# First projection of an encoder trunk: keys, values and the first q group in one pass of 512 columns

## The chip, the cores and the metric

The kernel runs on one core of a Trainium2 chip. Its time is the device time of one execution in microseconds; lower is better. Matmuls run on TensorE (PE, with its weight loads as PEld), elementwise work on VectorE (DVE), ScalarE (ACT) and GpSimd (POOL); nearly all transfers are issued by SyncE (SP).

## The reference, cut to what matters

Two sequences (1024 and 512 tokens, width 1024) go through the same two layers. Only the beginning of layer 0 is changed:

```
z = rmsnorm(x, g) @ w_in          # qa 512 | ka 128 | va 128 | ga 512 | mixer B 1536 columns
qa = rotate_pairs(rmsnorm(qa per head, gain0), ang) * 64**-0.5    # 8 heads of 64
ka = rotate_pairs(rmsnorm(ka per head, gain1), ang)               # 2 heads of 64
oa = dense_gqa(qa, ka, va)        # per sequence, 4 query heads share a key head
ob = rmsnorm(retention forwards + backwards of the mixer B columns)
x  = x + concat(silu(ga) * oa, silu(gb) * ob) @ w_out
```

Layer 1 has windowed attention with its own projections, and a last RMSNorm follows. Everything is float32.

## The kernel before, in words

The 1536 tokens are 12 blocks of 128, in three groups (t = 0, 1, 2) of four; group 2 is the second sequence. x arrives transposed: for each group t and each k of 8 pieces of the width there is a tile of 128 features by 512 tokens. `load_xt` scales it by g and splits it into a rounded part `xh` (ACT; POOL for group 2) and a rest `xl` (DVE, L118). The norm's factor `rs` (one per token) does not depend on the projection: `block_stats` (L388) reads x a second time, sums squares on ACT (L177), and takes the power on POOL (L103); `rs` is multiplied in when results leave PSUM, or later.

Weights come in chunks of 256 columns (`CW`). `load_w` (L130) loads two k of a chunk at once (128 x 512, rows of 2 KB), and POOL splits each such tile into a rounded part (L139) and a rest (L140), so a chunk is four tiles. They live in two sets of four slots, tags "w" and "wg"; their raw form has two slots (`wraw`), or, for the first chunk, slots of the general tag "E" (12).

A projection `proj_tm_k` (L150) of one block and one k is three matmuls into PSUM: xh by the weights' rounded part, xh by their rest, xl by their rounded part. The tokens are the stationary operand, the weights' 256 columns move.

The order around the change:

1. Chunk 4 (keys and values, 256 columns) is loaded into "w", beside x of group 0, then x of groups 1 and 2, then chunk 5 (the first q group, four heads) into "wg".
2. L450: for each group four PSUM banks, k outside, the four blocks inside; ACT copies the result without `rs` to `zkv` tiles (two blocks each, six in all); then the group's `block_stats`.
3. The rotary tables: one for q is written to DRAM (`tabq_d`), one for keys (`rk`) stays. Then chunk 0, the retention's first weights, is loaded into "w".
4. `q_pieces_a(0, ...)` (L465): for each of the six pairs of blocks one bank, k inside, into two halves of 256 columns. ACT multiplies by `rs` (L476), and SP writes q to DRAM (`q_d`, L481). Between the pairs stand `kv_pair` (L496: multiplies keys and values by `rs`, then `rope_norm`, L418: Square on ACT, sum on DVE, power on POOL, three products on DVE and POOL, a sum) and, after two pairs, `kv_group` (L503: PE transposes the keys, `ptk`; keys and values are split and written to DRAM, L519).
5. The retention (L571), head by head: each head's chunk is projected (`psb`, 256 columns, three PSUM banks in turn), rotated (DVE L588, POOL L590), transposed (`ptq`), and so on. The next head's chunk is loaded ahead, the second one into "wg". Behind each half `q_late` (L484) reads a pair of q from DRAM, norms and rotates it, and writes it back.
6. The attention of mixer A, with gates and the second q group as filler, and the rest.

Each engine works through its instructions in order, and so does SP with its transfers. The order on each is set when the kernel is built: a planner takes the program's order as priority, simulates the engines, and lets a ready instruction pass one that still waits. A tile's slot is free when its last reader is done.

Of the kernel before, what the change touches and what calls it, by code (L numbers as in the profile page):

```python
# [8 lines left out]
F32 = mybir.dt.float32  # L9
# [7 lines left out]
P = 128  # L17
# [19 lines left out]
def trunk_kernel(ctx, tc, x, xT, wab, woab, wc, woc, gT, qkg, ret, sink, relb, fng,  # L37
# [15 lines left out]
    def buf(tag, name, n=None, dt=F32):  # L53
        t = wk.tile([P, SIZE[tag]], dt, tag=tag, name=name, bufs=BUFS[tag])
        return t if n is None else t[:, :n]
# [9 lines left out]
    def ps_p(name, use="fill"):  # L65
        free = ring[use]
        ring["i"] = next(i % 3 for i in range(ring["i"] + 1, ring["i"] + 4) if i % 3 in free)
        return pp.tile([P, 512], F32, tag=f"pj{ring['i']}", name=name, bufs=1)
# [26 lines left out]
    def bcast(ap, n):  # L95
        return bass.AP(ap.tensor, ap.offset, [[0, P], [1, n]])
# [33 lines left out]
    def load_w(arr, c, tag, lo=None, hook=None, ks=range(KT), raws=None):  # L130
        ts = {}
        for i in (k // 2 for k in ks[::2]):
            if raws is None:
                raw = wp.tile([P, 2 * CW], F32, tag="wraw", name="wraw", bufs=2)
                dma(out=raw, in_=arr[c, :, 2 * i:2 * i + 2, :].rearrange("p k n -> p (k n)"))
            else:
                raw = raws[i]
            w = wp.tile([P, 2, 2 * CW], F32R, tag=tag, name=tag, bufs=4)
            nc.gpsimd.tensor_scalar(w[:, 0, :], raw, 1.0, 1.0, ALU.mult, ALU.mult)  # L139
            (lo or nc.gpsimd).tensor_tensor(w[:, 1, :], raw, w[:, 0, :].bitcast(F32), ALU.subtract)  # L140
            ts[i] = w
            if hook is not None:
                hook(i)

        def get(s, k, a=0, n=CW):
            o = (k % 2) * CW + a
            return ts[k // 2][:, s, o:o + n]
        return get

    def proj_tm_k(ps, w, b, k, ks=range(KT)):  # L150
        t, o = b // GB, (b % GB) * P
        xh, xl = X["h", k, t][:, o:o + P], X["l", k, t][:, o:o + P]
        mm(ps, xh, w(0, k), k == ks[0], False)
        mm(ps, xh, w(1, k), False, False)
        mm(ps, xl, w(0, k), False, k == ks[-1])
# [97 lines left out]
    def stage(name):  # L253
        s = wp.tile([P, 2, 2 * CW], F32R, tag="wg", name=name, bufs=4)
        return s[:, 0, :].bitcast(F32), s[:, 1, :].bitcast(F32)
# [124 lines left out]
    def fetch_xt(t, k):  # L380
        xt = buf("Q", "xt")
        dma(out=xt, in_=xT[k][:, t * 512:(t + 1) * 512])
        return xt

    def load_xt(t, k, xt=None):
        split_x(fetch_xt(t, k) if xt is None else xt, k, t, g_sb[:, k:k + 1], t == 2)

    def block_stats(t):  # L388
        for b in range(t * GB, t * GB + GB):
            block_rstd(load_block(x[b], "xb", "H"), rs[:, b:b + 1])  # L390
# [1 line left out]

    nc.scalar.dma_start(out=g_sb, in_=gT)
    nc.scalar.activation(rs, rs, AF.Tanh)
    raws, xts = [], []
    for i in range(KT // 2):
        raws.append(buf("E", "wraw"))
        dma(out=raws[i], in_=wab[4, :, 2 * i:2 * i + 2, :].rearrange("p k n -> p (k n)"))
        xts += [fetch_xt(0, 2 * i), fetch_xt(0, 2 * i + 1)]
    wkv = load_w(wab, 4, "w", None, lambda i: [load_xt(0, k, xts[k]) for k in (2 * i, 2 * i + 1)], raws=raws)  # L400
    for t in range(1, NG):
        for k in range(KT):
            load_xt(t, k)
    wq0 = load_w(wab, 5, "wg")

    def rope_table(i):
        tab = buf("S4", "tab").rearrange("p (f b d) -> p f b d", f=2, b=8)
        dma(out=tab, in_=ropeA)
        qk = buf("E", "qkg_s", 128)
        dma(out=qk, in_=bcast(qkg[i:i + 1], 128))  # L410
        if i == 0:
            nc.vector.tensor_scalar(qk, qk, 0.125, None, ALU.mult)
        for f in range(2):
            nc.vector.tensor_tensor(tab[:, f], tab[:, f], qk[:, f * 64:f * 64 + 64].unsqueeze(1)
                                    .to_broadcast([P, 8, 64]), ALU.mult)
        return tab

    def rope_norm(z, tb, nh, pos, tab):  # L418
        tb = tb.rearrange("p (b h d) -> p b h d", b=2, h=nh)
        nc.scalar.activation(tb, z, AF.Square)  # L420
        ss = small("ssa", 8)[:, :2 * nh]
        nc.vector.tensor_reduce(ss.rearrange("p (b h) -> p b h", b=2), tb, AX.X, ALU.add)
        r = rstd_of(ss, 64, 2 * nh).rearrange("p (b h) -> p b h", b=2)
        nc.vector.tensor_tensor(z, z, r.unsqueeze(3).to_broadcast([P, 2, nh, 64]), ALU.mult)
        cosb, sinb = tab[:, 0, pos:pos + 2, :], tab[:, 1, pos:pos + 2, :]
        for f in range(2):
            nc.gpsimd.tensor_tensor(
                tb[:, :, :, f * 32:f * 32 + 32], z[:, :, :, (1 - f) * 32:(2 - f) * 32],
                sinb[:, :, f * 32:f * 32 + 32].unsqueeze(2).to_broadcast([P, 2, nh, 32]), ALU.mult)
        nc.vector.tensor_tensor(z, z, cosb.unsqueeze(2).to_broadcast([P, 2, nh, 64]), ALU.mult)  # L430
        nc.vector.tensor_tensor(z, z, tb, ALU.add)
# [15 lines left out]
        nc.gpsimd.dma_start(out=pair[i], in_=sp_d[name, 1, i])  # L447

    kv_raw = []
    for t in range(NG):  # L450
        pss = [(ps_any if t == 1 and j < 3 else ps_s)("pskv")[:, :CW] for j in range(GB)]
        for k in range(KT):
            for j in range(GB):
                proj_tm_k(pss[j], wkv, t * GB + j, k)
        for j in range(0, GB, 2):
            z = buf("E", "zkv")
            for i in range(2):
                nc.scalar.activation(z[:, i * CW:(i + 1) * CW], pss[j + i], AF.Copy)
            kv_raw.append(z.rearrange("p (b s h d) -> p b s h d", b=2, s=2, h=2))
        block_stats(t)  # L460
    dma(out=tabq_d, in_=rope_table(0))
    rk = rope_table(1)
    ws = [load_w(wab, 0, "w")]

    def q_pieces_a(g, w, tab, filler):  # L465
        for p in PAIRS if filler else range(NB // 2):
            b = 2 * p
            ps = (ps_p if filler else ps_any)("psq")
            for j in range(2):
                for k in range(KT):  # L470
                    proj_tm_k(ps[:, j * CW:(j + 1) * CW], w, b + j, k)
                    if k % 2 and (j, k) != (1, KT - 1):
                        yield
            z, tb = stage("zq") if filler else (buf("E", "zq"), None)
            for j in range(2):
                nc.scalar.activation(z[:, j * CW:(j + 1) * CW], ps[:, j * CW:(j + 1) * CW], AF.Copy,  # L476
                                     scale=rs[:, b + j:b + j + 1])
            if filler:
                rope_norm(z.rearrange("p (b h d) -> p b h d", b=2, h=4), tb, 4, b % 8, tab)
            for j in range(2):  # L480
                dma(out=q_d[g][b + j], in_=z[:, j * CW:(j + 1) * CW])  # L481
            yield

    def q_late(p):  # L484

        z, tb = buf("E", "zq"), buf("H", "tbq")
        for j in range(2):
            dma(out=z[:, j * CW:(j + 1) * CW], in_=q_d[0][2 * p + j])
        tab = buf("Q", "tabs", 256).rearrange("p (f b d) -> p f b d", f=2, b=2)
        pos = (2 * p) % 8  # L490
        dma(out=tab, in_=tabq_d[:, :, pos:pos + 2, :])
        rope_norm(z.rearrange("p (b h d) -> p b h d", b=2, h=4), tb, 4, 0, tab)
        for j in range(2):
            dma(out=q_d[0][2 * p + j], in_=z[:, j * CW:(j + 1) * CW])

    def kv_pair(p):  # L496
        z = kv_raw[p]
        for j in range(2):
            nc.scalar.activation(z[:, j], z[:, j], AF.Copy, scale=rs[:, 2 * p + j:2 * p + j + 1])
        k = z[:, :, 0]  # L500
        rope_norm(k, buf("H", "tbk", 256), 2, (2 * p) % 8, rk)

    def kv_group(t):  # L503
# [6 lines left out]
        for i in range(2):  # L510
# [7 lines left out]
            for n, v in (("ak", ks[i]), ("av", vs[i])):  # L518
                dma(out=group((sp_d[n, i, 0], sp_d[n, i, 1]), t), in_=v.bitcast(F32))  # L519

    dma(out=lg, in_=bcast(ret, 8))
    nc.scalar.activation(lg, lg, AF.Exp)
    nc.vector.tensor_scalar(lg, lg, -1.0, None, ALU.mult)
# [11 lines left out]
    for h in range(4):  # L535
        nc.vector.tensor_scalar(mrel[:, h], dist_s[:, 0], lg[:, h:h + 1], None, ALU.mult)
        nc.vector.scalar_tensor_tensor(mrel[:, h], dist_s[:, 1], lg[:, 4 + h:5 + h], mrel[:, h], ALU.mult, ALU.add)
        nc.scalar.activation(mrel[:, h], mrel[:, h], AF.Exp)
    q0 = q_pieces_a(0, wq0, None, False)
    for p in range(NB // 2):  # L540
        for _ in range(8):
            next(q0)
        kv_pair(p)
        if p % 2:
            kv_group(p // 2)


    ropeb = buf("S4", "ropeb").rearrange("p (f b d) -> p f b d", f=2, b=8)
# [252 lines left out]
            nc.scalar.activation(group(R, t), ps, AF.Copy)  # L801

    def fill_a():
        yield from q_pieces_a(1, load_w(wab, 6, "w"), rq1, True)
        rbuild()
        bias_table()
        yield from gate_stream(wab, 7, g_ab, lambda t: group(R, t))
# [386 lines left out]
```

## Time and profile before

| | us |
|---|---|
| three runs | 1503.12, 1508.62, 1507.78 (median 1507.78) |
| the profiled execution | 1507.83 |
| its span, first to last instruction | 1506.1 |
| PE busy in the span | 1451.7 (96%) |
| DVE / ACT / POOL busy | 1052.6 / 719.5 / 812.3 |

Busy time is counted per instruction; matmuls overlap in the pipe, so a PE that is busy throughout says that matmuls follow each other, not how fast. For the pace one takes the starts of neighbouring matmuls. "Idle before" names how long an engine stood before an instruction, and what released it. 8734 matmuls run in all; the 576 of the changed projection take place in the first 80 us.

### The profile page before, as it was taken

What the parts mean: (1) busy time and instruction counts of PE and PEld (TensorE: products, weight loads), DVE (VectorE), ACT (ScalarE), POOL (GpSimd) and SP (SyncE); (2) the same over time, 40 slices, a digit from 0 to 9 for tenths busy, and PEclk for the clock granted to TensorE, in tenths of its full rate; (3) what the DMA queues carried; (4) which work ended last, traced back from release to release, by engine and by line L of the source; (5) the groups of instructions that cost most, each with busy time, mean ns of one, the idle gap of its engine ahead of it and who ended that gap; (6) DMA issues with size and microseconds to landing.
All of it is one profiled execution on the core that took longest, in us unless ns stands there. A gap on an engine that the chain in (4) does not pass through costs nothing.

```text
span 1506.1 us, 26020 instructions
## 1 busy us (share of the span) xinstructions
PE 1451.7 (96%) x8734; PEld 1269.8 (84%) x8734; DVE 1052.6 (70%) x2431; ACT 719.5 (48%) x1770; POOL 812.3 (54%) x1044
## 2 busy tenths in 40 slices
PE   8999999989999999999999999999999999999997
PEld 8989999977888888777778998888888888777777
DVE  7455867686676666887978237687777767888774
ACT  5632222354555555555653245566556556645202
POOL 7654654474645484887887423342522532566542
PEclk9999999999999999999999999999999999999999
DMA  9631212326212143643664231121212211568752
GB/s 329 207 119 51 75 54 69 99 74 191 74 45 72 53 113 116 206 141 107 192 213 141 86 109 46 61 71 50 74 45 94 63 54 53 173 206 280 229 157 99
DMA packets 137333, 176.59 MB, mean 117 GB/s; under 512 B 38064, under 2 KB 66736, under 8 KB 137200
## 3 DMA queue, kind: packets, MB, share of 16 engines
q1 hardware_dynamic: 135040, 169.41, 35.8%
q0 software_dynamic: 2016, 5.51, 1.3%
q8 instruction: 69, 1.13, 0.3%
q14 instruction: 64, 0.52, 0.1%
q10 hardware_dynamic: 144, 0.01, 0.0%
HBM read 125.83 MB, written 53.25 MB: 119 GB/s over the span
## 4 chain that ended last, share of the span: by engine, by line
PE 71%; DVE 11%; DMA 4%; POOL 4%; issue 3%; ACT 1%; SPq 0%; POOLq 0%; DVEq 0%; ACTq 0%
PE psg L89 17%; PE psq L89 10%; PE po L89 8%; PE psb L89 8%; PE pso L89 8%; PE pte L173 7%; PE s L89 4%; PE sc L89 4%; PE pskv L89 2%; DVE xl L118 2%; DVE w L140 1%; DVE el L112 1%; DMA wraw<-in_woc 1%; DVE nm L837 1%; PE ptq L173 1%
## 5 line engine op out<-in xcount | busy, mean ns | idle before, releaser
L89 PE MATMUL psg<-xh,wg 128*128 128x512 f32 x768 | 263.9, 400 | 0.2 <-POOL wg L140 0.2
L107 POOL TENSOR_SCALAR ec<-ec,rl 128x384 f32<-128x384 f32 (+1 forms) x192 | 108.8, 581 | 241.5 <-DVE rl L1056 87.7
L112 DVE TENSOR_TENSOR el<-pte,eh 128x512 fp32r<-128x512 f32 x288 | 196.6, 685 | 56.2 <-ACT eh L111 32.5
L111 ACT ACTIVATE eh<-pte 128x512 fp32r<-128x512 f32 x288 | 170.1, 596 | 119.7 <-PE po L89 65.0
L89 PE MATMUL pso<-xh,w 128*128 128x512 f32 x512 | 183.6, 418 | 10.4 <-DVE w L140 4.6
L89 PEld LDWEIGHTS psg<-xh,wg 128*128 128x128 f32 x768 | 143.9, 189 | 29.2 <-POOL e L107 0.9
L107 POOL TENSOR_SCALAR e<-e,rl 128x512 f32<-128x512 f32 x160 | 114.3, 726 | 93.3 <-DVE rl L848 33.9
L89 PE MATMUL psg<-xl,wg 128*128 128x512 f32 x384 | 150.9, 393 | 0.0
L1051 ACT ACTIVATE ec<-ec,nm 128x384 f32<-128x384 f32 (+1 forms) x192 | 109.6, 572 | 82.7 <-DVE nm L1049 77.7
L845 ACT ACTIVATE e<-s,nm 128x512 f32<-128x512 f32 x160 | 108.9, 687 | 68.0 <-DVE nm L842 50.0
L837 DVE TENSOR_REDUCE nm<-s 128x1 f32<-128x512 f32 x160 | 107.8, 683 | 37.4 <-PE s L89 36.9
L139 POOL TENSOR_SCALAR w<-wraw 128x512 fp32r<-128x512 f32 x116 | 79.4, 686 | 97.6 <-PE pskv L89 32.4
L89 PE MATMUL psq<-xh,w 128*128 128x512 f32 x384 | 130.0, 397 | 0.0
L89 PEld LDWEIGHTS pso<-xh,w 128*128 128x128 f32 x512 | 99.4, 197 | 35.8 <-DVE w L140 7.8
L1045 DVE CUSTOM_DVE_ANT_0 ec<-sc,bias,sink_s 128x384 f32<-128x384 f32 (+1 forms) x192 | 105.3, 568 | 22.2 <-PE sc L89 17.8
L89 PE MATMUL pso<-xl,w 128*128 128x512 f32 x256 | 104.1, 408 | 2.0 <-DVE xl L118 2.0
L173 PE MATMUL pte<-ident,e 128*128 128x128 f32 x640 | 96.0, 275 | 1.6 <-POOL e L107 0.8
L173 PEld LDWEIGHTS pte<-ident,e 128*128 128x128 f32 x640 | 78.8, 142 | 20.3 <-ACT e L845 2.2
L140 POOL TENSOR_TENSOR w<-wraw,w 128x512 fp32r<-128x512 f32 x68 | 91.2, 1344 | 1.9
L89 PEld LDWEIGHTS psg<-xl,wg 128*128 128x128 f32 x384 | 72.5, 189 | 13.1
L89 PEld LDWEIGHTS psq<-xh,w 128*128 128x128 f32 x384 | 71.9, 188 | 13.6
L173 PE MATMUL pte<-ident,ec 128*128 128x128 f32 x512 | 79.0, 272 | 0.2
(230 smaller groups left out, 3942.6 us busy)
## 6 DMA issues: line engine op xcount, KB each, us to landing
wraw<-in_woab SPq DMA_DIRECT2D x48, 256.0 KB, 3.4
wraw<-in_woc SPq DMA_DIRECT2D x48, 256.0 KB, 3.8
wraw<-in_wab SPq DMA_DIRECT2D x44, 256.0 KB, 3.3
wraw<-in_wc SPq DMA_DIRECT2D x36, 256.0 KB, 3.1
xt<-in_xT SPq DMA_DIRECT2D x24, 256.0 KB, 5.4
xb<-in_x SPq DMA_DIRECT2D x24, 256.0 KB, 4.8
qd<-qd SPq DMA_DIRECT2D x48, 128.0 KB, 2.9
gab<-gz SPq DMA_DIRECT2D x24, 256.0 KB, 2.0
```

The lines of the kernel that those rows point to most:

```text
L89: i = nc.tensor.matmul(ps, lhsT=lhsT, rhs=rhs, start=start, stop=stop)
L107: nc.gpsimd.tensor_scalar(o, i, s, 1.0, ALU.mult, ALU.mult)
L111: nc.scalar.activation(hi, src, AF.Copy)
L112: nc.vector.tensor_tensor(lo, src, hi.bitcast(F32), ALU.subtract)
L118: nc.vector.scalar_tensor_tensor(lo, src, scale, hi.bitcast(F32), ALU.mult, ALU.subtract)
L139: nc.gpsimd.tensor_scalar(w[:, 0, :], raw, 1.0, 1.0, ALU.mult, ALU.mult)
L140: (lo or nc.gpsimd).tensor_tensor(w[:, 1, :], raw, w[:, 0, :].bitcast(F32), ALU.subtract)
L173: return nc.tensor.transpose(o, i, ident)
L837: nc.vector.tensor_reduce(nm2[:, c:c + 1] if nh == 2 else nm[:, h:h + 1], s, AX.X, ALU.max, negate=True)
L845: nc.scalar.activation(eh[c], ss[c], AF.Exp, bias=nm[:, h:h + 1], accum_out=l[:, h, c:c + 1])
L1045: nc.vector.tensor_tensor_reduce(es[h][:, :nk], s, bias[h][:, bo:bo + nk], 1.0, sink_s[:, 4 * c + h:4 * c + h + 1], ALU.add, ALU.max, mx[: ...
L1051: nc.scalar.activation(es[a][:, :nk], es[a][:, :nk], AF.Exp, bias=nm[:, a:a + 1], accum_out=l[:, a:a + 1])
```

## The change

Chunks 4 and 5 are loaded together: tile k holds the 256 columns of both for one k (two rows of 1 KB each per partition instead of one of 2 KB), and is split by POOL into a tile of 512 columns; tiles k = 0 to 3 take the "w" slots, k = 4 to 7 the "wg" slots. `project(t)` makes keys, values and q of a group in one pass: k outside, four blocks inside, three matmuls of 512 columns into one bank per block. ACT copies each half of a bank without `rs`, and q is written to DRAM so; `q_late` now multiplies by `rs`, with two more ACT instructions. `q_pieces_a` remains for the second q group only. The order becomes: x of groups 0 and 1, project(0), statistics of group 0, x of group 2, tables, statistics of groups 1 and 2, the load of the retention's first chunk, project(1), the keys of group 0, project(2), the keys of groups 1 and 2.

```diff
-    raws, xts = [], []
-    for i in range(KT // 2):
+    raws, xts, wkq = [], [], []
+    for k in range(KT):
         raws.append(buf("E", "wraw"))
-        dma(out=raws[i], in_=wab[4, :, 2 * i:2 * i + 2, :].rearrange("p k n -> p (k n)"))
-        xts += [fetch_xt(0, 2 * i), fetch_xt(0, 2 * i + 1)]
-    wkv = load_w(wab, 4, "w", None, lambda i: [load_xt(0, k, xts[k]) for k in (2 * i, 2 * i + 1)], raws=raws)
-    for t in range(1, NG):
-        for k in range(KT):
-            load_xt(t, k)
-    wq0 = load_w(wab, 5, "wg")
+        dma(out=raws[k].rearrange("p (c n) -> p c n", c=2), in_=wab[4:6, :, k, :].rearrange("c p n -> p c n"))
+        xts.append(fetch_xt(0, k))
+    for k in range(KT):
+        w = wp.tile([P, 2, 2 * CW], F32R, tag="w" if k < 4 else "wg", name="wkq", bufs=4)
+        nc.gpsimd.tensor_scalar(w[:, 0, :], raws[k], 1.0, 1.0, ALU.mult, ALU.mult)
+        nc.gpsimd.tensor_tensor(w[:, 1, :], raws[k], w[:, 0, :].bitcast(F32), ALU.subtract)
+        wkq.append(w)
+        load_xt(0, k, xts[k])
+    for k in range(KT):
+        load_xt(1, k)
...
-    for t in range(NG):
-        pss = [(ps_any if t == 1 and j < 3 else ps_s)("pskv")[:, :CW] for j in range(GB)]
+
+    def project(t):
+
+        pss = [(ps_any if t == 1 and j < 3 else ps_s)("pskq") for j in range(GB)]
         for k in range(KT):
             for j in range(GB):
-                proj_tm_k(pss[j], wkv, t * GB + j, k)
+                proj_tm_k(pss[j], lambda s_, k_: wkq[k_][:, s_, :], t * GB + j, k)
         for j in range(0, GB, 2):
-            z = buf("E", "zkv")
+            z, zq = buf("E", "zkv"), buf("E", "zq")
             for i in range(2):
-                nc.scalar.activation(z[:, i * CW:(i + 1) * CW], pss[j + i], AF.Copy)
+                nc.scalar.activation(z[:, i * CW:(i + 1) * CW], pss[j + i][:, :CW], AF.Copy)
+                nc.scalar.activation(zq[:, i * CW:(i + 1) * CW], pss[j + i][:, CW:], AF.Copy)
+                dma(out=q_d[0][t * GB + j + i], in_=zq[:, i * CW:(i + 1) * CW])
             kv_raw.append(z.rearrange("p (b s h d) -> p b s h d", b=2, s=2, h=2))
-        block_stats(t)
-    dma(out=tabq_d, in_=rope_table(0))
-    rk = rope_table(1)
-    ws = [load_w(wab, 0, "w")]
...
             dma(out=z[:, j * CW:(j + 1) * CW], in_=q_d[0][2 * p + j])
+            nc.scalar.activation(z[:, j * CW:(j + 1) * CW], z[:, j * CW:(j + 1) * CW], AF.Copy,
+                                 scale=rs[:, 2 * p + j:2 * p + j + 1])
...
+    project(0)
+    block_stats(0)
+    for k in range(KT):
+        load_xt(2, k)
+    dma(out=tabq_d, in_=rope_table(0))
+    rk = rope_table(1)
+    block_stats(1)
+    block_stats(2)
+    ws = [load_w(wab, 0, "w")]
     dma(out=lg, in_=bcast(ret, 8))
...
-    q0 = q_pieces_a(0, wq0, None, False)
-    for p in range(NB // 2):
-        for _ in range(8):
-            next(q0)
+    project(1)
+    for p in range(2):
         kv_pair(p)
-        if p % 2:
-            kv_group(p // 2)
+    kv_group(0)
+    project(2)
+    for t in range(1, NG):
+        for p in range(2 * t, 2 * t + 2):
+            kv_pair(p)
+        kv_group(t)
```

## Rows read from the trace of the kernel before

**Rows 1.** The page: busy time, share of the span and instructions by engine.

```profile
PE 1451.7 (96%) x8734; PEld 1269.8 (84%) x8734; DVE 1052.6 (70%) x2431; ACT 719.5 (48%) x1770; POOL 812.3 (54%) x1044
```

**Rows 2.** Windows: length, busy time and instructions by engine, granted clock, DMA.

```profile
10.00:76.00 66.00, 66.00 (x548) 66.00 (x547) 40.90 (x81) 41.67 (x115) 45.14 (x57) 1.00 0.78 266
76.00:100.00 24.00, 20.63 (x170) 20.02 (x168) 14.91 (x34) 8.56 (x24) 15.88 (x26) 1.00 0.56 182
```

**Rows 3.** Timeline of PE from its first matmul: start, us, instructions merged.

```profile
6.53 2.05 PE L89 MATMUL pskv<-w,xh 128*128 128x256 f32 x8 [6.53 <-ACT xh L117]
...
11.49 1.12 PE L89 MATMUL pskv<-w,xh 128*128 128x256 f32 x8
```

**Rows 4.** The chain that ended last (256 columns); PE's timeline far later (512).

```profile
105.24 8.87 PE psb L89 x74
...
1399.96 0.39 PE L89 MATMUL pso<-xl,w 128*128 128x512 f32 x1
...
1402.68 0.39 PE L89 MATMUL pso<-xl,w 128*128 128x512 f32 x1
```

**Rows 5.** Waits of PE from 76 to 105 us: total, times, longest.

```profile
PE ptk L173 <- DVE zkv L431: 2.0, 2, 1.0
PE ptq L173 <- DVE qk L595: 1.6, 1, 1.6
```

**Rows 6.** Timeline at 78 us, then the chain from 88 to 100 us.

```profile
78.58 0.40 PE L89 MATMUL psb<-w,xh 128*128 128x256 f32 x2
78.66 0.63 POOL L139 TENSOR_SCALAR wg<-wraw 128x512 fp32r<-128x512 f32 x1
...
88.63 5.42 DMA wraw<-in_wab
...
94.19 0.75 POOL wg L139
...
95.03 1.29 POOL wg L140
96.32 0.59 POOL wg L139
...
98.28 1.12 POOL tb L590 x4
```

**Rows 7.** Timeline of POOL and DVE: splits of weights and of x.

```profile
5.01 0.62 POOL L139 TENSOR_SCALAR w<-wraw 128x512 fp32r<-128x512 f32 x1 [3.71 <-DMA wraw<-in_wab]
5.72 1.27 POOL L140 TENSOR_TENSOR w<-wraw,w 128x512 fp32r<-128x512 f32 x1
...
9.66 1.06 POOL L139 TENSOR_SCALAR w<-wraw 128x512 fp32r<-128x512 f32 x1
10.81 1.60 POOL L140 TENSOR_TENSOR w<-wraw,w 128x512 fp32r<-128x512 f32 x1
12.38 1.06 POOL L139 TENSOR_SCALAR w<-wraw 128x512 fp32r<-128x512 f32 x1
...
6.42 11.61 DVE L118 SCALAR_TENSOR_TENSOR xl<-xt,g_sb,xh 128x512 fp32r<-128x512 f32 x10 [5.52 <-ACT xh L117]
...
24.16 1.42 DVE L118 SCALAR_TENSOR_TENSOR xl<-xt,g_sb,xh 128x512 fp32r<-128x512 f32 x2 [0.79 <-ACT xh L117]
```

**Rows 8.** Timeline: first Square and last sum of the keys' norm and rotation.

```profile
64.20 0.41 ACT L420 ACTIVATE tbk<-zkv 128x256 f32<-128x256 f32 x1
...
86.52 0.42 DVE L431 TENSOR_TENSOR zkv<-zkv,tbk 128x256 f32<-128x256 f32 x1
```

**Rows 9.** DMA rate in 40 slices: 68 to 70 us (q's writes), 8 to 20 us.

```profile
GB/s 0 0 0 0 0 0 0 0 0 0 0 0 0 0 0 164 328 348 348 389 328 348 185 144 82 205 287 410 348 328 328 328 205 123 21 0 0 0 0 0
...
GB/s 389 376 396 376 341 348 341 355 376 396 403 389 416 382 389 403 389 389 382 341 294 294 266 280 294 212 164 205 232 362 335 280 341 369 376 403 417 416 369 423
```

**Rows 10.** A window of the retention; the scaling of keys and values on ACT.

```profile
160.00:180.00 20.00, 20.00 (x174) 20.00 (x173) 15.23 (x32) 5.67 (x11) 12.81 (x21) 1.00 0.34 93
...
L499 ACT ACTIVATE zkv<-zkv,rs 128x256 f32<-128x256 f32 x12 | 6.1, 506 | 3.5 <-POOL rs L103 3.4
```

More of the change, by code (lines that the diff above doesn't have):

```diff
@@ L449, in trunk_kernel, with q_pieces_a @@
     kv_raw = []
-    for t in range(NG):
-        pss = [(ps_any if t == 1 and j < 3 else ps_s)("pskv")[:, :CW] for j in range(GB)]
+    def project(t):
+        pss = [(ps_any if t == 1 and j < 3 else ps_s)("pskq") for j in range(GB)]
         for k in range(KT):
             for j in range(GB):
-                proj_tm_k(pss[j], wkv, t * GB + j, k)
+                proj_tm_k(pss[j], lambda s_, k_: wkq[k_][:, s_, :], t * GB + j, k)
         for j in range(0, GB, 2):
-            z = buf("E", "zkv")
+            z, zq = buf("E", "zkv"), buf("E", "zq")
             for i in range(2):
-                nc.scalar.activation(z[:, i * CW:(i + 1) * CW], pss[j + i], AF.Copy)
+                nc.scalar.activation(z[:, i * CW:(i + 1) * CW], pss[j + i][:, :CW], AF.Copy)
+                nc.scalar.activation(zq[:, i * CW:(i + 1) * CW], pss[j + i][:, CW:], AF.Copy)
+                dma(out=q_d[0][t * GB + j + i], in_=zq[:, i * CW:(i + 1) * CW])
             kv_raw.append(z.rearrange("p (b s h d) -> p b s h d", b=2, s=2, h=2))
-        block_stats(t)
-    dma(out=tabq_d, in_=rope_table(0))
-    rk = rope_table(1)
-    ws = [load_w(wab, 0, "w")]
-    def q_pieces_a(g, w, tab, filler):
-        for p in PAIRS if filler else range(NB // 2):
+    def q_pieces_a(g, w, tab):
+        for p in PAIRS:
             b = 2 * p
-            ps = (ps_p if filler else ps_any)("psq")
+            ps = ps_p("psq")
             for j in range(2):
@@ L473, in q_pieces_a @@
                         yield
-            z, tb = stage("zq") if filler else (buf("E", "zq"), None)
+            z, tb = stage("zq")
             for j in range(2):
@@ L477, in q_pieces_a @@
                                      scale=rs[:, b + j:b + j + 1])
-            if filler:
-                rope_norm(z.rearrange("p (b h d) -> p b h d", b=2, h=4), tb, 4, b % 8, tab)
+            rope_norm(z.rearrange("p (b h d) -> p b h d", b=2, h=4), tb, 4, b % 8, tab)
             for j in range(2):
@@ L803, in fill_a @@
     def fill_a():
-        yield from q_pieces_a(1, load_w(wab, 6, "w"), rq1, True)
+        yield from q_pieces_a(1, load_w(wab, 6, "w"), rq1)
         rbuild()
```

## The prediction

> **What bounds the kernel now.** I read the page first: TensorE (PE) is busy for 1451.7 us, 96% of the span [rows 1], so the time of the stage that is changed must be read from that stage. The windows come next: from 10 to 76 us PE is busy throughout, from 76 to 100 us it is idle for 3.4 us, and both at a granted clock of 1.00, the 2.4 GHz level [rows 2]. A busy PE says little of its pace, so I read starts. In the steady stretch 74 matmuls of 256 columns take 8.87 us, 119.9 ns each [rows 4]. The first 24 are slower: 6.53 to 11.49 us, 207 ns each, though the rows grant the full clock there [rows 3]; I don't decide why. From there 552 more at 119.9 ns give 77.7 us, and the retention's first matmul (psb) starts at 78.58 us [rows 6]; the difference is the key transposes in between. So this stage is paced by PE alone, and what comes behind is, too: from 160 to 180 us PE shows no idle time [rows 10]. A microsecond saved before 78.58 us should reach the end.
>
> **The change part by part.** My base is the profiled execution, 1507.83 us by the device clock (its span is 1506.1); the median of the three runs shown, 1507.78, is the same for this purpose.
>
> *Matmuls.* 288 for keys and values and 288 for the first q, 256 columns each, become 288 of 512 columns. Nothing of 512 columns runs in this stage, but later stages show it: from 1399.96 to 1402.68 us there are 12 starts, 226.7 ns each [rows 4]. Two narrow ones take 239.8 ns, so 13.1 ns go per wide matmul: 288 x 13.1 = 3.8 us. Both widths cost about 13 ns over their columns at 2.4 GHz (256/2.4 = 106.7, 512/2.4 = 213.3), which is why half the matmuls save half the overhead.
> The Trainium skill (TensorE: Matmul & The Clock Gate, section Back-to-back issue gap) puts the fixed part at about 2.5 ns; by that figure the saving is an estimated 0.7 us. The rows have five times as much, and I go by them.
>
> *The beginning.* The first weight load is as large as before and nothing new precedes it, so I leave the start at 6.53 us, and the slow stretch at 4.96 us; it now holds 12 wide matmuls, all of k = 0. Then 276 at 226.7 ns: the groups of blocks end at 30.5, 52.3 and 74.1 us, 3.6 to 3.8 us earlier than the 77.7 above.
>
> *POOL feeds it.* Each k now needs its own weight tile, split by POOL in two instructions. They take 0.62 + 1.27 us with VectorE (DVE) idle and 1.06 + 1.60 us beside its splits, with the gaps 2.72 us for a tile [rows 7]. PE eats a tile in 12 x 0.2267 = 2.72 us. That is a tie, with POOL a tile ahead: eight tiles are done at 5.0 + 8 x 2.72 = 26.8 us, and PE reaches the eighth at 27.8. I count it at nothing. If POOL were 0.5 us slower per tile, PE would lose up to 3 us. Before, one tile served 24 matmuls (2.88 us), so the balance is as tight but lasts twice as long.
>
> *DMA.* Eight weight loads of 256 KB replace four and four: as many issues on SP. Their rows shrink from 2 KB to 1 KB. The trace moves 1 KB rows (q's writes) at 328 to 348 GB/s in most of their full slices, and mostly 2 KB ones at 376 to 416 [rows 9]. The 2 MB cost some 6.2 instead of 5.3 us, and a weight and an x piece together 1.5 us per k, beside PE's 2.72: hidden. The last x pieces for group 2 move behind group 0's statistics; they are needed at 52 us, and the queue has 22 us for 4 MB.
>
> *ScalarE (ACT).* The evacuations are as many. Added are 12 scalings in q_late, by the nearest row 0.51 us each, 6.1 us [rows 10]. They stand on ACT behind the read of q that the Square there waited for already, so no new wait arises; behind them stand the retention's evacuations. ACT is busy 5.7 of 20 us there [rows 10]: nothing, with 6.1 us as the bound if all of it stood on the path. q's writes come earlier, and their reader is unchanged.
>
> *Slots.* The eight weight tiles hold all "w" and "wg" slots until the third group has passed each k. The retention's first weights wait for "w": free at 52.3 + 2.7, 5.4, 8.2 and 10.9 us, so by 63.2. Two of their raw loads are early; the other two follow the splits of these, 5.4 us each at worst [rows 6], so the four tiles are ready by about 70, ahead of 74.1. The second set waits for "wg", now free one by one from 65.9 to 74.1 us. Before, all four came free only with the last q matmul, and the splits began at 78.66 [rows 6].
>
> *Behind the projection.* Before, PE waited 2.0 us for key transposes and 1.6 us for the first retention transpose [rows 5]. The chain behind the latter: two raw loads issued at 88.63 us, 5.42 us to land, POOL's splits to 98.28, only then the rotary products that stood behind them on POOL, then qk [rows 6]. With "wg" free earlier this chain can start up to 10 us earlier, so the 1.6 us can go; but SP reaches these loads only after writes that wait for the keys, and the last keys are now there only at 74.1 us, with the end of the pass. The key chain itself ran from 64.20 to 86.9 us in the old kernel [rows 8], held up by what came before it rather than by its input, so I expect its end within a few us of that. The bounds are -3.6 us (all three waits go) and +3.6 (as much again); I take -0.9, half of the 1.6.
>
> Sum: -3.8 - 0.9 = -4.7, 1503.1 us.
>
> **The rivals.**
> *All the waits go.* If POOL has both weight sets split and the keys done while three free banks keep PE in psb (144 matmuls, 17.3 us), the gain is 3.8 + 3.6 = 7.4: 1500.4 us. For it: the release k by k. Against it: the transposes of group 2 are placed in PE's order by a planner, and PE stood a whole us at two of them [rows 5] although their inputs were projected long before.
> *POOL and DVE exclude each other.* DVE's 16 splits of groups 0 and 1 take 1.16 us each beside POOL and 0.71 without it [rows 7]. If the two could not overlap at all, 8 x 1.94 (0.62 + 1.27, with gaps) + 16 x 0.71 = 26.9 us of work would end at 31.9 and group 0 at 34.6 us, 4.1 late: 1507.2. Against it: together they did a tile and 2.3 splits in 2.72 us, where in turn these take 3.6, so they overlap in part.
> That rule is the Trainium skill's (SBUF — State Buffer, Who interferes with whom): a DVE instruction with two SBUF inputs and a GpSimd one that reads SBUF block each other whole. The slowing agrees with it, its size does not.
> *The matmul overhead doesn't shrink.* If a wide matmul with weights as moving operand costs what two narrow ones do less 2.5 ns (a transfer the late stages, with x moving, can't rule out), 0.7 + 0.9 us go: 1506.2. All 512-column groups of the trace hold this pace, so it is unlikely.
> *Slower: the retention's weights come late.* All slots being held, the third and fourth raw loads for the retention's first weights wait on SP and POOL in order. If SP sits before a write that waits for a later result, as it did until 88.63, they are issued only when the projection ends. A load takes 5.42 us to land, the two splits 0.75 + 1.29 and some 0.59 + 1.29 [rows 6], 9.3 in all; PE can do 12 matmuls (1.4 us) on the first two tiles and 6 (0.7 us) on the third, so it loses 7.2: 1507.8 + 7.2 - 3.8 = 1511.2. It decides when that issue is later than 74.1 - 7.2 = 66.9 us, and each us beyond 74.1 adds one. For it: exactly this happened to the next set. Against it: by the slots the issue is due some 7 us before that.
>
> **How the numbers follow.** Chances: forecast 0.45 (own range 1499 to 1507), all waits gone 0.18, POOL and DVE 0.12, overhead kept 0.08, weights late 0.17. The range 1496 to 1513 takes in all of these up to half of the last, and the unknown of a planner that orders the rest anew. Half a per cent, 7.5 us, is about what a measurement of this kernel can tell from no change: faster means under 1500.3, slower over 1515.3. Faster: half of the second case, and a fifth of the first's lower side, 0.18. Slower: the half of the last in which the issue is some 4 us later still, 0.09. The same: 0.73.
>
> **What would show it.** 288 pskq matmuls at about 227 ns, the third group's last near 74 us, show the main term; 235 ns or more would halve it. POOL's eighth split ending by 28 us, and PE without a gap at 30.5 and 52.3, show the feeding right. The retention's first weights split before 74 us, and the idle time of PE in the 25 us after it, decide the rest. If psb starts later than 78.6 the prediction is wrong in its first term; if it starts at 74 and the end doesn't move, my claim that PE paces all behind it is wrong.

## The result, and the profile after

The changed kernel takes 1517.47 us (median of five, 1515.61 to 1519.02) against 1507.78 for the kernel before on the same chip (1503.12 to 1510.67): ratio 1.0062, 95% interval 1.0049 to 1.0076. It is slower by 9.7 us, where a gain of 4.7 was forecast, and lies outside the forecast range of 1496 to 1513. The profiled execution is the fastest of the five, 1515.61 us, with a span of 1513.8.

The page, row by row as in [rows 1]:

```profile
PE 1446.4 (96%) x8446; PEld 1250.3 (83%) x8446; DVE 1049.5 (69%) x2431; ACT 723.5 (48%) x1782; POOL 813.3 (54%) x1044
```

288 matmuls fewer, PE busy 5.3 us less, and yet a longer span: the time went into waiting. The windows of [rows 2] again (length, busy time and instructions of PE, PEld, DVE, ACT, POOL, then granted clock, DMA share and GB/s):

```profile
10.00:76.00 66.00, 49.87 (x212) 40.80 (x212) 38.17 (x81) 38.27 (x106) 40.51 (x49) 0.87 0.72 249
76.00:100.00 24.00, 24.00 (x139) 21.15 (x138) 8.23 (x20) 8.84 (x28) 16.59 (x19) 1.00 0.58 174
```

The projection, which had no hole before, has one of 16.1 us, and the stretch behind it has lost its 3.4. PE's waits from 0 to 120 us (total, times, longest), beside [rows 5]:

```profile
PE ptk L173 <- DVE zkv L434: 16.1, 1, 16.1
PE pskq L89 <- ACT xh L117: 5.7, 1, 5.7
```

One wait, at the transposes of group 0's keys. PE's timeline shows its place (start, us, operation; in brackets the idle time before it):

```profile
5.74 3.75 PE L89 MATMUL pskq<-wkq,xh 128*128 128x512 f32 x8 [5.74 <-ACT xh L117]
9.29 1.78 PE L89 MATMUL pskq<-wkq,xl 128*128 128x512 f32 x4
10.90 1.32 PE L89 MATMUL pskq<-wkq,xh 128*128 128x512 f32 x5
...
51.52 0.39 PE L89 MATMUL pskq<-wkq,xl 128*128 128x512 f32 x1
68.04 0.66 PE L173 MATMUL ptk<-ident,zkv 128*128 128x128 f32 x2 [16.13 <-DVE zkv L434]
68.35 1.20 PE L89 MATMUL pskq<-wkq,xh 128*128 128x512 f32 x2
69.35 0.63 PE L89 MATMUL pskq<-wkq,xl 128*128 128x512 f32 x1
69.78 1.05 PE L89 MATMUL pskq<-wkq,xh 128*128 128x512 f32 x2
70.63 0.63 PE L89 MATMUL pskq<-wkq,xl 128*128 128x512 f32 x1
71.06 1.05 PE L89 MATMUL pskq<-wkq,xh 128*128 128x512 f32 x2
71.91 0.54 PE L89 MATMUL pskq<-wkq,xl 128*128 128x512 f32 x1
72.29 0.62 PE L89 MATMUL pskq<-wkq,xh 128*128 128x512 f32 x2
...
92.60 0.48 PE L89 MATMUL psb<-w,xh 128*128 128x256 f32 x2
```

Two transposes stand directly behind the second group's last matmul, and 96 matmuls of the third group, whose inputs are there, stand behind them. What the transposes waited for, on the timelines of SP's queue, ACT, DVE and POOL:

```profile
28.69 0.51 ACT L503 ACTIVATE zkv<-zkv,rs 128x256 f32<-128x256 f32 x1
...
30.76 0.54 ACT L503 ACTIVATE zkv<-zkv,rs 128x256 f32<-128x256 f32 x1
...
57.01 0.94 SPq L198 DMA_DIRECT2D xb<-in_x  x2
...
59.69 0.19 ACT L177 ACTIVATION_READ_ACCUMULATOR junk<-xb 128x1 f32 x1
59.79 0.71 ACT L423 ACTIVATE tbk<-zkv 128x256 f32<-128x256 f32 x2
60.24 0.73 DVE L425 TENSOR_REDUCE ssa<-tbk 128x4 f32<-128x256 f32 x2
...
61.24 0.61 ACT L177 ACTIVATE junk<-xb 128x512 f32<-128x512 f32 x1
...
62.47 0.55 POOL L103 TENSOR_TENSOR rs<-ms,nhalf 128x1 f32<-128x1 f32 x1 [1.52 <-DVE ms L100]
62.99 2.97 POOL L103 TENSOR_TENSOR rstd<-ms,nhalf 128x4 f32<-128x4 f32 x3
...
67.47 0.42 DVE L434 TENSOR_TENSOR zkv<-zkv,tbk 128x256 f32<-128x256 f32 x1
```

The first Square of the keys (L423) starts at 59.79 us, behind 22 of the 24 sums of squares of the statistics (L177), and POOL takes the keys' power (rstd) only behind the last rs. Its own input was there long before: ACT had scaled the two blocks of the first pair at 28.69 and 30.76 (L503). What holds it is its place on ACT behind sums that wait in part for loads of x (3.5 us before the one at 42.97), none of which it needs. In the kernel before, the same Square stood at 64.20 [rows 8], just as late. But there PE came to the transposes at 74.01, when the keys had been done for 1.5 us, and did not wait (timelines of DVE and PE):

```profile
72.07 0.42 DVE L431 TENSOR_TENSOR zkv<-zkv,tbk 128x256 f32<-128x256 f32 x1
...
74.01 0.38 PE L173 MATMUL ptk<-ident,zkv 128*128 128x128 f32 x2
```

So the chain didn't get later; PE got to it 22 us earlier. Before, PE started the last matmul for keys and values at 45.57 us and went on with q's matmuls, none of which waited, until the keys were done. The change has put those matmuls into the passes.

From the two timelines the retention's first matmul moves from 78.58 [rows 6] to 92.60, by 14.0 us: the start is 0.8 earlier, the wait is 16.1, nine matmuls after it run at half pace (1.9, below), and the rest is the width: 276 matmuls at 13.1 ns less, 3.6 us: -0.8 + 16.1 + 1.9 - 3.6 = 13.6 of the 14.0. Then 4.1 us come back: the first matmul of the second q group (psq) moves by 9.9 (265.25 to 275.15). The old waits of 3.6 us [rows 5] are gone; that what they waited for had 14 us more is the likely reason. The difference is 10.0 at the first psq of layer 1 (512 columns, 890.5 to 900.5), 7.7 in the two spans and 9.7 in the medians.

### The profile page after: what moved, and what is told of

Read it like the earlier page. It is cut to its first block, busy times and chain, and to the rows that moved or that the text cites. A ratio compares the mean times of both kernels' runs of the same rounds, so it can differ in the third digit from the quotient of the medians.

```text
span 1513.8 us, 25436 instructions
## 1 busy us (share of the span) xinstructions
PE 1446.4 (96%) x8446; PEld 1250.3 (83%) x8446; DVE 1049.5 (69%) x2431; ACT 723.5 (48%) x1782; POOL 813.3 (54%) x1044
## 4 chain that ended last, share of the span: by engine, by line
PE 73%; DVE 11%; DMA 6%; POOL 4%; issue 3%; ACT 2%; SPq 0%; POOLq 0%; DVEq 0%; ACTq 0%
PE psg L89 17%; PE psq L89 10%; PE psb L89 9%; PE po L89 8%; PE pso L89 8%; PE pte L173 6%; PE sc L89 3%; PE s L89 3%; PE pskq L89 3%; PE pskv L89 2%; DVE xl L118 2%; DMA wraw<-in_woc 2%; DVE w L140 1%; DVE el L112 1%; DVE nm L852 1%
## 5 line engine op out<-in xcount | busy, mean ns | idle before, releaser
L89 PE MATMUL pso<-xh,w 128*128 128x512 f32 x512 | 179.1, 408 | 8.7 <-DVE w L140 4.5
L139 POOL TENSOR_SCALAR w<-wraw 128x512 fp32r<-128x512 f32 x112 | 76.1, 680 | 92.1 <-PE pskv L89 32.1
L140 POOL TENSOR_TENSOR w<-wraw,w 128x512 fp32r<-128x512 f32 x64 | 85.3, 1336 | 1.8
L89 PEld LDWEIGHTS psq<-xh,w 128*128 128x128 f32 x384 | 71.9, 188 | 13.6
```

The costliest lines, as they stand in the source:

```text
L89: i = nc.tensor.matmul(ps, lhsT=lhsT, rhs=rhs, start=start, stop=stop)
```

## The experiments

All are timed in five rounds beside the kernel before, and each ratio is to it. The wait is PE's for ptk up to 110 us, psb the start of the retention's first matmul, both in the profiled execution.

| kernel | wait, us | psb, us | median, us | ratio, 95% interval |
|---|---|---|---|---|
| before | 2.0 | 78.6 | 1507.8 | 1 |
| changed | 16.1 | 92.6 | 1517.5 | 1.0062 (1.0049 to 1.0076) |
| 1 keys after project(2) | 2.6 | 72.8 | 1503.8 | 0.9973 (0.9961 to 0.9984) |
| 2 own slots | 16.6 | 93.2 | 1517.7 | 1.0067 (1.0055 to 1.0079) |
| 3 chain first | 2.5 | 74.5 | 1502.2 | 0.9965 (0.9952 to 0.9978) |
| 4 as 1, 256 columns | 1.0 | 77.8 | 1504.0 | 0.9972 (0.9961 to 0.9983) |
| 5 only the transposes after | 2.5 | 73.6 | 1503.3 | 0.9970 (0.9954 to 0.9986) |
| 6 as 3, no scaling of q | 2.3 | 74.5 | 1502.2 | 0.9957 (0.9940 to 0.9974) |
| 7 both moves | 1.9 | 74.0 | 1499.8 | 0.9941 (0.9917 to 0.9964) |
| 8 half way | 7.1 | 83.2 | 1508.9 | 1.0006 (0.9991 to 1.0020) |
| 9 as 7, 256 columns | 0.4 | 77.5 | 1503.4 | 0.9967 (0.9954 to 0.9979) |
| 10 as 7, again | 1.4 | 73.9 | 1499.1 | 0.9948 (0.9929 to 0.9966) |
| 11 as 7, second pairs early | 1.1 | 72.8 | 1499.7 | 0.9946 (0.9930 to 0.9963) |

1 to 4, 5 to 8 and 9 to 11 ran together. psb also carries the start of the program: the first matmul behind k = 0 begins between 9.9 us (kernel 11) and 11.5 us (kernel 4), because PE's first start lies between 5.5 and 6.2 us and the clock rises at different times (last section). So 1.6 us at psb can have nothing to do with an edit.

**1. All of group 0's key work behind the third projection.**

```diff
     project(1)
+    project(2)
-    for p in range(2):
-        kv_pair(p)
-    kv_group(0)
-    project(2)
-    for t in range(1, NG):
+    for t in range(NG):
```

> The keys of group 0 (kv_pair 0 and 1, kv_group 0) stand behind project(2) in the program; nothing else differs from the changed kernel. Theory A (PE stands in order behind the first key transpose, placed ahead of project(2), whose input comes 16.1 us too late; this wait and the slow matmuls behind it are the whole loss): no wait of PE over 3 us before the first psb, which starts at 74 to 76 us instead of 92.6; the time falls by 13 to 17 us to 1500 to 1504. Theory B (the late work has to be waited for anyway: statistics, keys and the retention's first weights): PE waits some 10 us or more at psb or soon behind it, the time stays at 1510 or above.

The hole is gone. The waits of PE up to 125 us, and a window of this kernel that has 24 us busy where the changed one has 7.96:

```profile
PE pskq L89 <- ACT xh L117: 5.8, 1, 5.8
PE ptk L173 <- DVE zkv L434: 2.6, 2, 2.2
```

```profile
52.00:76.00 24.00, 23.93 (x118) 20.14 (x117) 9.97 (x28) 14.44 (x44) 20.34 (x27) 1.00 0.48 142
```

With the same weights, slots and widths the kernel is faster than before. The loss is the place of this work in the order. (psb came at 72.8, before the 74 to 76 expected.)

**2. The Square's output in a slot of its own.** In the changed kernel the tiles `tbk` share the four slots of tag "H" with the statistics' loads.

```diff
-        rope_norm(k, buf("H", "tbk", 256), 2, (2 * p) % 8, rk)
+        rope_norm(k, buf("O", "tbk", 256), 2, (2 * p) % 8, rk)
```

> The order of the program stays; only the square of the keys' norm (tbk) takes its slot from another tag (O, two slots) than the one in which the x blocks of the statistics rotate (H, four slots). Theory A1 (the keys' chain is late because its square waits for a slot behind the x blocks of groups 1 and 2): the first square runs at 45 to 50 us instead of 59.8, the wait of PE at the first key transpose falls from 16.1 to under 4 us, the time to 1501 to 1506. Theory A2 (it is late because POOL and DVE work in order behind the last block's statistics, whatever the slot): the square comes early, but the transpose still waits over 10 us; the time stays at 1514 or above.

Nothing gets earlier, on ACT's timeline neither:

```profile
61.29 0.63 ACT L177 ACTIVATE junk<-xb 128x512 f32<-128x512 f32 x1 [0.26 <-DMA xb<-in_x]
61.82 0.19 ACT L177 ACTIVATION_READ_ACCUMULATOR junk<-xb 128x1 f32 x1
61.92 0.71 ACT L423 ACTIVATE tbk<-zkv 128x256 f32<-128x256 f32 x2
```

The Square stands behind the last sum of squares with slots to spare: not the slots hold it but the order on ACT and POOL. I had looked for an earlier Square that then waits on POOL; ACT's own order holds it too.

**3. The first two kv_pair ahead of the second group's statistics.** The transposes stay ahead of project(2).

```diff
     rk = rope_table(1)
+    for p in range(2):
+        kv_pair(p)
     block_stats(1)
...
     project(1)
-    for p in range(2):
-        kv_pair(p)
     kv_group(0)
```

> kv_pair 0 and 1 stand ahead of the statistics of groups 1 and 2 in the program, so that the keys' chain goes first on every engine; kv_group 0 stays ahead of project(2). By theory A (both A1 and A2) the transpose of group 0 finds its input at about 52 us: a wait under 3 us, 1500 to 1505. If the rotary table for the keys (done on DVE at 43.9 us) or the load of x for group 2 holds the chain up, a wait of 3 to 8 us stays, 1506 to 1512. By theory B 1510 or above.

The Squares now stand at 33.77 and 40.42 on ACT, the keys' last sum on DVE is done at 49.25, and the four transposes follow the second group's last matmul without a wait (timelines of ACT, DVE and PE):

```profile
33.77 0.42 ACT L423 ACTIVATE tbk<-zkv 128x256 f32<-128x256 f32 x1
40.42 0.42 ACT L423 ACTIVATE tbk<-zkv 128x256 f32<-128x256 f32 x1
...
48.83 0.42 DVE L434 TENSOR_TENSOR zkv<-zkv,tbk 128x256 f32<-128x256 f32 x1
...
52.30 0.60 PE L173 MATMUL ptk<-ident,zkv 128*128 128x128 f32 x4
```

1 moves the waiting instruction, 3 what it waits for; either removes the hole, so it is the two together.

**4 and 9. The projection in halves of 256 columns again**, all but k = 0, 276 matmuls more: 4 on the kernel of experiment 1, 9 on that of 7.

```diff
-                proj_tm_k(pss[j], lambda s_, k_: wkq[k_][:, s_, :], t * GB + j, k)
...
+                    for x_, s_ in ((xh, 0), (xh, 1), (xl, 0)):
+                        for c in range(2):
+                            h = slice(c * CW, (c + 1) * CW)
+                            mm(pss[j][:, h], x_, wkq[k][:, s_, h], False, k == KT - 1 and x_ is xl and c == 1)
```

> As e1_keys_after, but all matmuls of the pass except those of k = 0 are cut into two halves of 256 columns: 276 more matmuls, the same loads, splits and order of the program. If 13.1 ns go per matmul saved, as the rows before show: the pass is 3.6 us longer than that of e1_keys_after, and the time 3 to 4 us above it. If only 2.5 ns go (the Trainium skill, TensorE: Matmul & The Clock Gate, section Back-to-back issue gap): 0.7 us. If the pass is not paced by PE: no difference.

> The kernel with both moves, its projection in two halves of 256 columns again (all but k = 0, so 276 matmuls more), against the same kernel at 512 columns run beside it. Theory A (each narrow pair costs 13.1 ns more, and PE paces all behind the projection): psb begins 3.6 us later (77.6), and the end is 3 to 4 us later. Rival (what the width gains before psb is given back in the retention's waits, as the small difference of the first pair of kernels, 0.2 us of the medians, would say): psb 3.6 later, the end 0 to 1.5 later.

In 4 psb begins 4.9 us later than in 1; 1.2 of it is there at the first matmul behind k = 0 (10.26 to 11.49), so 3.7 lie in the pass. In 9 psb moves from 73.9 (kernel 10, same chip) to 77.5, 3.6 us, 0.4 of it at the start, so 3.3 lie in the pass. 276 x 13.1 ns = 3.6 fits both. How much of this reaches the end the runs don't settle. From 1 to 4 the medians move by 0.2 us and the spans by 1.5; the waits for ptk behind psb shrank there from 2.6 to 1.0. From 10 to 9 the medians move by 4.3, from 7 (another set) by 3.6, and the spans by 2.0 and 1.3; the intervals of 9 overlap with those of 7 and 10. So the first pair speaks for the rival, the second for theory A. The pace, on the PE timelines of kernels 7 and 9 (six wide starts from 29.91 to 31.27 us; twelve narrow ones from 29.94 to 31.38):

```profile
29.91 0.39 PE L89 MATMUL pskq<-wkq,xl 128*128 128x512 f32 x1
30.13 0.61 PE L89 MATMUL pskq<-wkq,xh 128*128 128x512 f32 x2
30.59 0.39 PE L89 MATMUL pskq<-wkq,xl 128*128 128x512 f32 x1
30.81 0.61 PE L89 MATMUL pskq<-wkq,xh 128*128 128x512 f32 x2
31.27 0.39 PE L89 MATMUL pskq<-wkq,xl 128*128 128x512 f32 x1
```

```profile
29.94 0.64 PE L89 MATMUL pskq<-wkq,xh 128*128 128x256 f32 x4
30.42 0.40 PE L89 MATMUL pskq<-wkq,xl 128*128 128x256 f32 x2
30.66 0.64 PE L89 MATMUL pskq<-wkq,xh 128*128 128x256 f32 x4
31.14 0.40 PE L89 MATMUL pskq<-wkq,xl 128*128 128x256 f32 x2
31.38 0.40 PE L89 MATMUL pskq<-wkq,xh 128*128 128x512 f32 x1
```

226.7 ns for a wide one, 120 for a narrow one, as [rows 4] had it from other stages. The Trainium skill (TensorE: Matmul & The Clock Gate, section Back-to-back issue gap) gives a single matmul's gap as 2.5 ns over its columns; by that figure the halves would cost an estimated 0.7 us. They cost 3.3 to 3.7 in the pass.

**5. Only the transposes moved** behind project(2); both kv_pair stay.

```diff
         kv_pair(p)
-    kv_group(0)
     project(2)
+    kv_group(0)
```

> From the changed kernel only the call that transposes the first group's keys (kv_group(0)) moves behind the third projection; the two scalings, norms and rotations of these keys (kv_pair) stay where they were. Theory A (what costs is the place of the four transposes in PE's order, nothing else of the two calls): as with all three calls moved: no wait over 3 us for ptk on PE between 10 and 92 us, psb begins at 72.5 to 74 us, 1503 to 1505 us. Rival A' (the place of kv_pair's work on ScalarE and GpSimd matters by itself, because it stands there ahead of the splits of the retention's weights): psb begins later than 75 us and the time is 1506 or more. Were it neither, the 16 us wait would still be there and the time 1517.

As in experiment 1 (wait 2.5, psb 73.6, 1503.3 us): of all that 1 moves, the place of the transposes on PE is enough.

**6. Without the scalings of q by rs**, else as kernel 3.

```diff
-            nc.scalar.activation(z[:, j * CW:(j + 1) * CW], z[:, j * CW:(j + 1) * CW], AF.Copy,
-                                 scale=rs[:, 2 * p + j:2 * p + j + 1])
```

> The kernel with the first keys' work placed ahead of the second block's statistics, less the 12 scalings of q by rs on ScalarE in q_late (so q of the first group isn't scaled by its row's norm: this part of the computation is left out). The prediction counted these scalings at nothing, with 6.1 us as the bound. Theory A (hidden): 1501.5 to 1503 us, as with them (1502.17), and psq's first start within 0.7 us of 260.5. Rival (they stand on the path): 1496 to 1499 us. A part of it, 1499 to 1501, would mean that some of the 12 delay the evacuations behind them.

1502.16 against 1502.17 us in the two sets, psq's first start 260.3 against 260.5. The 12 scalings, of which the changed kernel's trace counts 5.5 us, are hidden; the 6.1 us bound is out.

**7 and 10. Both moves**: kernel 3 with kv_group(0) behind project(2) as in 5.

> Both moves together: the first two kv_pair ahead of the second block's statistics, and the transposes of group 0 behind the third projection. Theory A (the waits for ptk of 2.5 us left with the first move alone lie at the key transposes near 92 us, of groups 1 and 2, and depend on the chains of these, not on group 0): waits of 2 to 3 us remain, psb begins at 72.5 to 73 us, 1501.5 to 1503.5 us, no gain over the one move alone (1502.17). Rival (with four transposes more in one place and their input ready, the planner has work to put into these waits): ptk waits under 1 us and 1499.5 to 1501.

> The kernel with both moves once more, as the other side of the two runs beside it: 1499 to 1501 us, ratio 0.993 to 0.9955. If the first result was the luck of that chip, it comes out at 1502 like the first move alone.

1499.8 and 1499.1 us, on two occasions: 0.5 to 0.6% faster than the kernel before, 1.2% than the changed one. A wait of 1.4 to 1.9 us stays, so the rival's reason for the gain (no wait) fails though its time came out; theory A's time failed, and psb (73.9 to 74.0) is later than it said. Against the one move of 3 the medians gain 2.4 to 3.1 us, with intervals that overlap, so a gain of the second move is likely and not shown; in the profiles 0.5 to 0.6 of it is there at psb and 1.2 to 1.7 at psq (260.5 to 259.3 and 258.8).

**8. Half way**: the two kv_pair between the second and the third group's statistics.

```diff
     block_stats(1)
+    for p in range(2):
+        kv_pair(p)
     block_stats(2)
...
     project(1)
-    for p in range(2):
-        kv_pair(p)
     kv_group(0)
```

> From the changed kernel only: the first two kv_pair stand between the statistics of the second and the third block instead of behind both; the transposes stay ahead of the third projection. In the changed kernel the Square stood behind the last of 24 sums of squares (61.2 us) and the transposes began 6.8 us after that. The sums of the second block end near 49 us there. Theory A (an in-order queue: the wait is as long as what stands ahead of the Square): transposes at 55 to 57 us, a wait of PE of 4 to 5.5 us in place of 16.1, psb begins at 78 to 81 us, and by the slope of the runs so far (14 us later at psb gave 9.6 us at the end against the 6 us of gain without a wait) 1505 to 1509 us. Rival (the wait hangs on the loads or on tabq, not on the statistics in front): still over 12 us and 1515 or more.

```profile
51.42 0.63 ACT L177 ACTIVATE junk<-xb 128x512 f32<-128x512 f32 x1
51.95 0.20 ACT L177 ACTIVATION_READ_ACCUMULATOR junk<-xb 128x1 f32 x1
52.04 0.41 ACT L423 ACTIVATE tbk<-zkv 128x256 f32<-128x256 f32 x1
...
59.16 0.66 PE L173 MATMUL ptk<-ident,zkv 128*128 128x128 f32 x2 [7.10 <-DVE zkv L434]
```

On the timelines of ACT and PE the Square comes at 52.0 instead of 59.8, the transposes at 59.2 instead of 68.0. The wait is 7.1 us where I had expected 4 to 5.5, psb 83.2 where I had expected 78 to 81. The wait follows what stands ahead of the Square, as the in-order queue has it; but I had placed the end of the second group's sums near 49 us, and the last of them starts at 52.87. The three kernels 3, 8 and changed are doses of one cause: waits of none, 7.1 and 16.1 us at this place, and 1502.2, 1508.9 and 1517.5 us. Each us of wait costs about 0.9 us at the end (by the ratios to before, of 1508 us: 6.2 for the first 7.1, 8.4 for the next 9.0, each give or take some 2 by the intervals).

**11. The second group's kv_pair ahead of project(2)**, to remove the last wait of kernel 7.

```diff
     project(1)
+    for p in range(2, 4):
+        kv_pair(p)
     project(2)
     kv_group(0)
-    for t in range(1, NG):
-        for p in range(2 * t, 2 * t + 2):
-            kv_pair(p)
-        kv_group(t)
+    kv_group(1)
+    for p in range(4, 6):
+        kv_pair(p)
+    kv_group(2)
```

> The kernel with both moves, and the second group's kv_pair (2 and 3) written ahead of the third projection, the transposes of groups 0 and 1 behind it. Theory A (the 1.9 us wait left at the transposes near 77.6 us hangs on pair 3's rotation, which stands late because it is written late): the wait goes and the time falls by 1 to 2 us, to 1498 to 1499. Rival (the rotation hangs on its own input, which comes with the last statistics, or on GpSimd's splits of the retention's weights, so an earlier place in the text changes nothing): wait 1.5 to 2.5, same time within 0.7 us.

Wait 1.1, 1499.7 us: no difference to 10 that these runs can tell; the 1.1 us that psb is earlier are there, but for 0.1, at the start (10.85 to 9.89). This leaves open what holds that rotation.

## Why the prediction was wrong

*The failed step* is in the part on the change: what the sum charges for the keys. "I expect its end within a few us of that" prices the end of the key chain, for all three groups, at 86.9 us, and "I take -0.9" what PE loses to it. The sum never asked where PE would stand when group 0's part of the chain ends. It had both numbers, and had even said that the chain is held up by what comes before it rather than by its input: PE ends the second group at 52.3 us, and the first Square is at 64.20 [rows 8], to which the chain then adds some 8 us (to 72.5 in the kernel before). Read together they say that transposes written between project(1) and project(2) wait, at worst until 72, 20 us; 16.1 came. Experiments 1, 3 and 5, which take away this wait and nothing else of the change, turn the loss into a gain. My bound on this place, "+3.6 (as much again)", was taken from old waits, not from the two positions.

The same paragraph asked the right question of the loads on SP (what is queued behind a late thing) and not of PE, although the diff takes kv_group(0) from among q's matmuls to a place ahead of project(2).

*Matmuls, -3.8:* right up to psb: 226.7 ns by the rows, 3.3 to 3.7 us in the pass for 276 (experiments 4 and 9). By the prediction's own timeline, which leaves the first 12 as slow as before, it is 276 x 13.1 = 3.6. That every microsecond before psb reaches the end is not shown: 0.2 us came of it in one pair, 3.6 to 4.3 in the other.

*The beginning:* the start moved from 6.53 to 5.74 where none was expected; why is open (the others began at 5.5 to 6.2). The first 12 took 5.16 us against 4.96. The reason for the slow stretch, which the prediction left open, is the clock (last section).

*POOL and DMA, 0:* right. PE ran from 5.74 to 51.9 us without idle time, and the eighth split was done at 24.6, by 28 as asked. DVE and POOL at full exclusion (1507.2 us) did not happen.

*ACT's scalings, 0:* right (experiment 6).

*Slots:* the retention's first weights were to be ready by about 70 and ahead of PE. They came at 73.24 and later, released by project(2)'s own matmuls, which stood 16 us late; psb found them ready at 92.6 (the first split, on POOL's timeline of the changed kernel):

```profile
73.24 0.62 POOL L139 TENSOR_SCALAR w<-wraw 128x512 fp32r<-128x512 f32 x1 [2.06 <-PE pskq L89]
```

With the hole removed, no wait for these weights shows either, so the slower rival (1511.2) had the sign and not the mechanism.

*Behind the projection, -0.9:* the prediction calls it half of the 1.6, which would be 0.8; either is a choice between its bounds. In the changed kernel the whole 3.6 came back, where all else had 14 us more. Without the hole (experiment 3) a wait of 2.5 us for ptk remains, and the 1.6 for ptq is gone. Kernel 3 is in effect what the sum described: psb 4.1 us earlier for 3.8, the old waits 1.1 shorter for 0.9, 1502.2 measured for 1503.1.

The sum with the missed term, by the rows after: -4.7 + 16.1 + 1.9 (half pace) = +13.3, less the 2.7 us more of old waits that vanish, 10.6; 9.7 were measured in the medians, 7.7 in the spans.

## What to carry to other kernels

For every step that moves across engines, put two times side by side: when the engine reaches the instruction in the new order, and when its input is ready by the chain that makes it; if the second is later, everything queued behind waits too. Work that is shortened or moved elsewhere may have been the cover of a late chain (here q's matmuls), so the chain is to be followed even when it isn't changed. Both cures are cheap, and either is enough: move the waiting instruction behind work that is ready (5), or move what it waits for ahead of what it doesn't need (3). The two together have the lowest medians (7 and 10).

## What the runs showed of the hardware

At its place a wait costs more than its length (at the end less, some 0.9 us for each, as the waits behind it shrink). After 16.1 us idle the changed kernel's PE starts six wide matmuls from 69.35 to 71.91 us at 427 ns each, where 226.7 is its pace; nine of them cost 1.9 us. The windows of the changed kernel, before, in and behind that stretch, have the granted clock in the third column from the right:

```profile
51.90:68.00 16.10, 0.01 (x1) 0.00 (x0) 6.02 (x25) 9.86 (x31) 7.73 (x12) 0.60 0.46 141
68.00:72.30 4.30, 4.26 (x12) 3.48 (x13) 3.80 (x7) 0.00 (x0) 3.17 (x6) 0.51 0.01 4
72.30:76.00 3.70, 3.70 (x19) 3.05 (x18) 0.00 (x0) 0.56 (x2) 1.92 (x2) 1.00 0.00 0
```

0.51 is the level of 1.2 GHz, where 512 columns take 426.7 ns. After the 7.1 us wait of kernel 8, six matmuls take 2.70 us instead of 1.36, 1.3 us more, with 0.66 granted from 59.2 to 63.5 us. The Trainium skill (TensorE: Matmul & The Clock Gate, section What's actually happening) says that an idle PE is put to the 1.2 GHz level; the trace agrees, the mean of 0.60 over the wait being a full clock that fell to half in the course of it.

The first matmuls of the program run no faster: eight start between 5.74 and 9.29 us, 444 ns each, and the view of this stretch prints the full clock beside them:

```profile
5.70:9.70 4.00, 3.96 (x9) 3.14 (x10) 2.51 (x3) 1.45 (x2) 3.83 (x5) 1.00 0.99 321
```

That 1.00 is no reading. The trace's list of clock grants has its first entry at 10.78 us, a rise to full, and the view counts the time before it as full. The starts agree with the list: 427 ns apart, but for the first two, up to 10.57 us, and 231 ns from 10.90 on. It is the same in all 13 traces: the first entry stands between 8.7 and 12.0 us, and the matmuls go over to full pace there. In the kernel before it is at 11.11 us, and the first narrow matmuls start 213 ns apart up to there, which are the slow 24 of [rows 3]; those rows hold no clock. So the first matmuls run at the 1.2 GHz level, and before the list's first entry the spacing of the starts is the reading to go by.

The spans differ by 2.3 us less than the starts of that psq do, 7.7 against 10.0. Matmul by matmul from the end, the difference falls between 1418 and 1448 us of the kernel before: it takes 29.2 us there for what the changed kernel does in 25.8, with 1.8 us more of idle time on PE and a granted clock of 0.94 for 1.00. Whether the change has any part in this, no run here tells.
